# A two-layer hybrid decoder trunk on one core: the first input split into high and low parts k-tile by k-tile, and lambda computed behind the indexer

## The chip, the cores and the metric

The kernel runs on one core of one Trainium2 chip. Five engines work side by side, each through its own queue in order: TensorE (PE, matmuls; its weight loads are shown as PEld), VectorE (DVE), ScalarE (ACT), GpSimd (POOL) and SyncE (SP, which issues most DMAs). The metric is the device time of one execution in microseconds (us), as the median of several runs; lower is better.

## The reference, cut to what matters

Two pre-norm residual layers over 256 tokens of width 1024, in float32. Layer 0 mixes with indexed sparse attention and differential attention, layer 1 with native sparse attention; each is followed by a SwiGLU block.

```python
h = rmsnorm(x, norm_mix[layer])                 # x: (1, 256, 1024)
y = h @ ev_w_in[j]                              # layer 0: one projection, split by columns
qa_nope, qa_rope, c_kv, ka_rope, iq, ik, iw, qb, kb, vb = split_cols(y, EVEN_SPLITS)
o_a = dsa_mixer(...)                            # indexer scores, top-64 keys, latent attention
o_b = diff_mixer(qb, kb, vb, ev_lambda[j], ev_subln[j], lam_init, pos)
x = x + concatenate([o_a, o_b]) @ ev_w_out[j]
x = x + swiglu(rmsnorm(x, norm_ffn[layer]), w_gate, w_up, w_down)
```

In diff_mixer one number per layer, `lam_full = exp(sum(l0*l1)) - exp(sum(l2*l3)) + lam_init`, weighs the second softmax against the first.

## The kernel before, in words

Every float32 product is made of three fp32r matmuls: an operand a is split into a high part (a rounded copy) and a low part (a minus the high part), and act_hi·w_hi, act_hi·w_lo and act_lo·w_hi are summed in one PSUM bank (`mm3`, L330 to L332). So each weight tile takes one ACT instruction for `w_hi` (L110) and one DVE instruction for `w_lo` (L113), in `Weights.prepare`. Weight tiles arrive by SP's queue in the order of use, and up to six split tiles stand ahead of TensorE.

The layer's first input `x` (two row tiles t = 0, 1 of 128 tokens; eight k-tiles of 128 columns) is transposed on TensorE, four k-tiles into one PSUM bank `pt_x` (there are two such banks), scaled by the norm's gain `gc0`, and split into `aW`. `first_half(t, h)` does this for one row tile and one half h of the k-tiles. For t = 0, h = 0 ACT and DVE work one k-tile at a time, straight from PSUM (L297, L298). For the three other halves DVE first writes the scaled half to SBUF as `xg` (L301, 512 columns), and ACT and DVE then split that (L240, L241). Behind it stand the sums of squares (L284, four on ACT), `rs` (L224 on DVE and a power on POOL, L225), and the first projection in chunks of 328, 416, 384 ... columns, in `project`: each chunk has four weight tiles of two k-tiles, so 48 matmuls. Each chunk's result is turned by `rope` (L390, L392, L395 on DVE).

The order on each engine is set by a scheduler that takes the program's order as priority and an instruction's readiness by its own costs; what is marked with `pin` (`keep_in_program_order`) keeps its place among the other pinned instructions of its engine. The scheduler also lets only one engine at a time at a PSUM bank, reads too: its waits are in the queue listings below as [waits ...].

`lam` (four small DVE instructions, L475, L476, L479 and L481, and one on ACT, L477) stands at the head of `even_mixer`. It is first used at L684, in differential attention.

Of the kernel before, what the change touches and what calls it, by code (L numbers as in the profile page):

```python
# [7 lines left out]
F32 = mybir.dt.float32  # L8
F32R = mybir.dt.float32r
BF16 = mybir.dt.bfloat16  # L10
AF = mybir.ActivationFunctionType
# [63 lines left out]
class Weights:  # L75
# [22 lines left out]
    def prepare(self, upto, behind=False):  # L98

        nc = self.tc.nc  # L100
        while len(self.ready) < min(upto, len(self.queue)):
            i = len(self.ready)
            self.load(i + 1)
            raw = self.raw[i]
            self.raw[i] = None
            _, kk, w = self.queue[i]
            n = kk * w
            hi = self.pool.tile([P, WCOLS], F32R, tag="hi", bufs=self.bufs[1], name="w_hi")
            lo = self.pool.tile([P, WCOLS], F32R, tag="lo", bufs=self.bufs[1], name="w_lo")
            act = nc.scalar.activation(hi[:, :n], raw[:, :n], AF.Copy)  # L110
            if behind:
                self.tc.keep_in_program_order(act)
            nc.vector.tensor_sub(lo[:, :n], raw[:, :n], hi[:, :n])  # L113
            self.ready.append((hi[:, :n].rearrange("p (k c) -> p k c", k=kk), lo[:, :n].rearrange("p (k c) -> p k c", k=kk)))

    def next(self, hold=1):
# [8 lines left out]
def trunk(tc, x, w0, w1, sm0, cw, vec, gcol, cst, out, dbg=None):  # L125
# [159 lines left out]
            if h == 1:  # L285
                rsqrt_sum(self.rs[t], ms)

    def first_half(nm, t, h):

        pt = t_bank("pt_x").rearrange("p (k c) -> p k c", k=4)  # L290
        for i in range(4):
            TE.transpose(pt[:, i], xs[t][:, (4 * h + i) * P : (4 * h + i + 1) * P], ident)
        hi, lo = nm.aT[t]
        if t == 0 and h == 0:
            for k in range(4):
                g = gc0[:, k : k + 1]
                pin(A.activation(hi[:, k], pt[:, k], AF.Copy, scale=g))  # L297
                V.scalar_tensor_tensor(lo[:, k], pt[:, k], g, hi[:, k], op0=ALU.mult, op1=ALU.subtract)  # L298
        else:
            xg = nat("xg").rearrange("p (k c) -> p k c", k=4)  # L300
            V.tensor_mul(xg, pt, gc0[:, 4 * h : 4 * h + 4].unsqueeze(2).broadcast_to([P, 4, P]))  # L301
            split(hi[:, 4 * h : 4 * h + 4], lo[:, 4 * h : 4 * h + 4], xg)

    class Final:

# [153 lines left out]
    def even_mixer(nm, goff):  # L459
        aT, rs = nm.aT, nm.rs  # L460
        with tc.tile_pool(name="even", bufs=1, reuse_waits="tile") as pool:
# [6 lines left out]
            ukT, uv = sm[:, :512], sm[:, 512:]  # L468


            lamv = small[:, V_LAM - V_KV :].rearrange("p (a b d) -> p a b d", a=2, b=2)
            lp = pool.tile([P, 2, 64], F32, tag="lam_p", name="lam_p")
            l2 = pool.tile([P, 2], F32, tag="lam_2", name="lam_2")
            nlam = pool.tile([P, 1], F32, tag="nlam", name="nlam")
            V.tensor_mul(lp, lamv[:, :, 0], lamv[:, :, 1])  # L475
            V.tensor_reduce(l2, lp, axis=AX.X, op=ALU.add)  # L476
            A.activation(l2, l2, AF.Exp)  # L477
            lam_init = 0.8 - 0.6 * math.exp(-0.3 * 0)
            V.tensor_scalar(nlam, l2[:, 1:2], l2[:, 0:1], -lam_init, op0=ALU.subtract, op1=ALU.add)  # L479
            subg = pool.tile([P, P], F32, tag="subg", name="subg")  # L480
            V.tensor_scalar(subg, small[:, V_SUB - V_KV : V_SUB - V_KV + P], 1.0 - lam_init, None, op0=ALU.mult)  # L481


            iTs = [early("iT").rearrange("p (k c) -> p k c", c=T) for _ in range(2)]
            iw_ = early("iw").rearrange("p (a t c) -> p a t c", a=2, t=NT)
            wv = [pool.tile([P, 8], F32, tag=f"wv{t}", name="wv") for t in range(NT)]
# [51 lines left out]
            for t in range(NT):  # L538
# [21 lines left out]
                V.tensor_scalar(am, work, TAKEN / 2, NEG, op0=ALU.is_gt, op1=ALU.mult)  # L560
                V.tensor_add(am, am, mask(t))
                addm.append(am)


            for h in range(0, 8, 4):
# [373 lines left out]
        return nxt  # L939

    first = Norm(V_MIX0)
    for h in range(2):
        for t in range(NT):
            first_half(first, t, h)
            W.prepare(2 * h + t + 1, behind=(h,t)==(0,1))
    for t in range(NT):
        for h in range(2):
            first.square(t, h)
# [135 lines left out]
```

## Time and profile before

| | |
|---|---|
| runs | 660.07, 664.07, 663.41 us; median 663.41 us |
| profiled execution | 661.37 us, of which the span from first to last instruction is 659.7 us |
| PE busy | 644.5 us (98% of the span) |
| DVE busy | 489.8 us (74%) |
| ACT busy | 396.8 us (60%) |

Busy time is the union of an engine's instructions. In a timeline row the first number is the start in us from the span's start, the second the time to the end of the last of the row's instructions; an engine's next instruction starts a little before the one ahead ends when it waits for nobody. What stands in square brackets is the idle time of that engine before the row and who ended it.

### The profile page before, as it was taken

What the parts mean: (1) busy time and instruction counts of PE and PEld (TensorE: products, weight loads), DVE (VectorE), ACT (ScalarE), POOL (GpSimd) and SP (SyncE); (2) the same over time, 40 slices, a digit from 0 to 9 for tenths busy, and PEclk for the clock granted to TensorE, in tenths of its full rate; (3) what the DMA queues carried; (4) which work ended last, traced back from release to release, by engine and by line L of the source; (5) the groups of instructions that cost most, each with busy time, mean ns of one, the idle gap of its engine ahead of it and who ended that gap; (6) DMA issues with size and microseconds to landing.
All of it is one profiled execution on the core that took longest, in us unless ns stands there. A gap on an engine that the chain in (4) does not pass through costs nothing.

```text
span 659.7 us, 10029 instructions
## 1 busy us (share of the span) xinstructions
PE 644.5 (98%) x3512; PEld 538.0 (82%) x3512; DVE 489.8 (74%) x1133; ACT 396.8 (60%) x804; POOL 12.9 (2%) x26
## 2 busy tenths in 40 slices
PE   8999999999999999999999999989999999999995
PEld 6978888788888888888888787766888888888884
DVE  5999977758978787544689889896698777775424
ACT  6785758547755555433377598786585555554312
POOL 2000000000000000000000000000000000000000
PEclk9999999999999999999999999999999999999998
DMA  8844354137866666663297420510486555565501
GB/s 296 297 126 155 96 179 142 32 138 258 255 192 189 188 191 190 191 193 104 68 376 234 144 101 12 163 61 1 165 277 201 188 191 191 182 184 187 194 21 65
DMA packets 31729, 109.15 MB, mean 165 GB/s; under 512 B 3648, under 2 KB 3904, under 8 KB 31424
## 3 DMA queue, kind: packets, MB, share of 16 engines
q1 hardware_dynamic: 31104, 107.92, 50.9%
q10 hardware_dynamic: 576, 0.59, 0.3%
q8 instruction: 28, 0.46, 0.3%
q14 instruction: 21, 0.17, 0.1%
HBM read 107.46 MB, written 1.05 MB: 164 GB/s over the span
## 4 chain that ended last, share of the span: by engine, by line
PE 85%; DVE 5%; ACT 3%; DMA 3%; issue 2%; POOL 0%; SPq 0%; POOLq 0%; ACTq 0%; DVEq 0%
PE ps_g L437 12%; PE ps_u L437 12%; PE ps_out L331 7%; PE ps_out L330 7%; PE ps_out L332 7%; PE ps_u L438 6%; PE ps_g L438 6%; PE ps_in L331 5%; PE ps_in L330 4%; PE ps_in L332 4%; DMA w_raw<-in_w 2%; PE ps_o L933 2%; PE pt_p L917 2%; DVE w_lo L113 2%; PE ps_s L898 1%
## 5 line engine op out<-in xcount | busy, mean ns | idle before, releaser
L113 DVE TENSOR_TENSOR w_lo<-w_raw,w_hi 128x1024 fp32r<-128x1024 f32 (+5 forms) x200 | 234.9, 1181 | 93.6 <-ACT w_hi L110 91.1
L110 ACT ACTIVATE w_hi<-w_raw 128x1024 fp32r<-128x1024 f32 (+5 forms) x200 | 203.5, 1023 | 136.0 <-PE ps_out L332 57.6
L437 PE MATMUL ps_g<-aW,w_hi 128*128 128x512 f32 x352 | 124.6, 396 | 0.3 <-DVE aW L241 0.3
L437 PE MATMUL ps_u<-aW,w_hi 128*128 128x512 f32 x352 | 124.6, 396 | 0.0
L438 PE MATMUL ps_u<-aW,w_lo 128*128 128x256 f32 x352 | 98.7, 280 | 0.0
L438 PE MATMUL ps_g<-aW,w_lo 128*128 128x256 f32 x352 | 98.7, 280 | 0.0
L437 PEld LDWEIGHTS ps_g<-aW,w_hi 128*128 128x128 f32 x352 | 66.0, 188 | 16.5 <-DVE aW L241 0.9
L437 PEld LDWEIGHTS ps_u<-aW,w_hi 128*128 128x128 f32 x352 | 66.0, 187 | 15.6 <-DVE hn L450 0.2
L330 PE MATMUL ps_in<-w_hi,aW 128*128 128x512 f32 (+5 forms) x208 | 76.9, 370 | 0.4 <-ACT aW L240 0.4
L331 PE MATMUL ps_in<-w_lo,aW 128*128 128x512 f32 (+5 forms) x208 | 77.0, 370 | 0.1
L332 PE MATMUL ps_in<-w_hi,aW 128*128 128x512 f32 (+5 forms) x208 | 76.0, 366 | 0.0
L331 PE MATMUL ps_out<-w_lo,hT_hi 128*128 128x512 f32 x176 | 69.2, 393 | 0.0
L332 PE MATMUL ps_out<-w_hi,hT_lo 128*128 128x512 f32 x176 | 69.0, 392 | 0.0
L330 PE MATMUL ps_out<-w_hi,hT_hi 128*128 128x512 f32 x176 | 68.7, 390 | 0.0
L438 PEld LDWEIGHTS ps_g<-aW,w_lo 128*128 128x128 f32 x352 | 66.5, 189 | 0.0
L438 PEld LDWEIGHTS ps_u<-aW,w_lo 128*128 128x128 f32 x352 | 66.5, 189 | 0.0
L400 ACT ACTIVATE e<-e,bias 128x128 f32<-128x128 f32 (+1 forms) x96 | 42.4, 446 | 2.6 <-DVE bias L399 2.6
L330 PEld LDWEIGHTS ps_in<-w_hi,aW 128*128 128x128 f32 x208 | 39.7, 191 | 4.8 <-ACT aW L240 0.6
L331 PEld LDWEIGHTS ps_in<-w_lo,aW 128*128 128x128 f32 x208 | 39.6, 190 | 4.7 <-issue 0.5
L332 PEld LDWEIGHTS ps_in<-w_hi,aW 128*128 128x128 f32 x208 | 39.5, 190 | 4.6 <-issue 0.5
L330 PEld LDWEIGHTS ps_out<-w_hi,hT_hi 128*128 128x128 f32 x176 | 33.0, 188 | 7.5
L331 PEld LDWEIGHTS ps_out<-w_lo,hT_hi 128*128 128x128 f32 x176 | 33.1, 188 | 7.0
(225 smaller groups left out, 892.4 us busy)
## 6 DMA issues: line engine op xcount, KB each, us to landing
w_raw<-in_w SPq DMA_DIRECT2D x176, 512.0 KB, 4.3
w_raw<-in_w SPq DMA_DIRECT2D x8, 384.0 KB, 4.5
gain<-in_vec SPq DMA_DIRECT2D x4, 512.0 KB, 4.6
cw<-in_cw SPq DMA_DIRECT2D x2, 1024.0 KB, 8.2
w_raw<-in_w SPq DMA_DIRECT2D x4, 416.0 KB, 5.3
w_raw<-in_w SPq DMA_DIRECT2D x4, 328.0 KB, 5.0
w_raw<-in_w SPq DMA_DIRECT2D x4, 304.0 KB, 2.7
x<-in_x SPq DMA_DIRECT2D x4, 256.0 KB, 5.1
```

Of the source, the lines that this page charges most:

```text
L110: act = nc.scalar.activation(hi[:, :n], raw[:, :n], AF.Copy)
L113: nc.vector.tensor_sub(lo[:, :n], raw[:, :n], hi[:, :n])
L330: TE.matmul(ps, act[0][:, k], wh, start=start, stop=False)
L331: TE.matmul(ps, act[0][:, k], wl, start=False, stop=False)
L332: TE.matmul(ps, act[1][:, k], wh, start=False, stop=stop)
L400: A.activation(e, e, AF.Exp, scale=-1.0, bias=bias, accum_out=den)
L437: TE.matmul(dst[f], wh[:, i, c], wide[:, k].rearrange("p z q -> p (z q)"), start=k == 0, stop=False)
L438: TE.matmul(dst[f][:, :T], wl[:, i, c], wide[:, k, 0], start=False, stop=k == KD - 1)
L898: mmi = TE.matmul(sb[:, i], qS[t][:, h], kz[:, par, :, :ns], start=z == 0, stop=z == 1)
L917: TE.transpose(pt[:, i, b, st], e[:, i, b, st * P : (st + 1) * P], ident)
L933: pin(TE.matmul(ob[64 * par : 64 * par + 64], vv[:, st, c : c + 64], pTs[par][:, b, st].rearrange("p j c -> p (j c)"), start=False, stop=l ...
```

## The change

The first input is split k-tile by k-tile in all four halves, from the transposes in PSUM; `xg` and the instructions L301, L240 and L241 go from this place. The transposes, the splits and the first four weight splits, on ACT and on DVE, are all pinned in a written order: tile 0, then t = 0 k-tiles 0 to 3, t = 1 k-tiles 0 and 1, weight tile 1, t = 1 k-tiles 2 and 3, and for the second half k-tiles 4 and 5 of both row tiles, weight tile 2, k-tiles 6 and 7 of both, weight tile 3. The sums of squares stand behind as before. The lambda instructions move from the head of `even_mixer` to behind the indexer.

```diff
-            act = nc.scalar.activation(hi[:, :n], raw[:, :n], AF.Copy)
+            parts = [nc.scalar.activation(hi[:, :n], raw[:, :n], AF.Copy), nc.vector.tensor_sub(lo[:, :n], raw[:, :n], hi[:, :n])]
             if behind:
-                self.tc.keep_in_program_order(act)
-            nc.vector.tensor_sub(lo[:, :n], raw[:, :n], hi[:, :n])
+                for part in parts:
+                    self.tc.keep_in_program_order(part)
...
-    def first_half(nm, t, h):
+    def first_turn(t, h):
 
         pt = t_bank("pt_x").rearrange("p (k c) -> p k c", k=4)
         for i in range(4):
-            TE.transpose(pt[:, i], xs[t][:, (4 * h + i) * P : (4 * h + i + 1) * P], ident)
+            pin(TE.transpose(pt[:, i], xs[t][:, (4 * h + i) * P : (4 * h + i + 1) * P], ident))
+        return pt
+
+    def first_split(nm, pt, t, h, ks):
+
         hi, lo = nm.aT[t]
-        if t == 0 and h == 0:
-            for k in range(4):
-                g = gc0[:, k : k + 1]
-                pin(A.activation(hi[:, k], pt[:, k], AF.Copy, scale=g))
-                V.scalar_tensor_tensor(lo[:, k], pt[:, k], g, hi[:, k], op0=ALU.mult, op1=ALU.subtract)
-        else:
-            xg = nat("xg").rearrange("p (k c) -> p k c", k=4)
-            V.tensor_mul(xg, pt, gc0[:, 4 * h : 4 * h + 4].unsqueeze(2).broadcast_to([P, 4, P]))
-            split(hi[:, 4 * h : 4 * h + 4], lo[:, 4 * h : 4 * h + 4], xg)
+        for i in ks:
+            k = 4 * h + i
+            g = gc0[:, k : k + 1]
+            pin(A.activation(hi[:, k], pt[:, i], AF.Copy, scale=g))
+            pin(V.scalar_tensor_tensor(lo[:, k], pt[:, i], g, hi[:, k], op0=ALU.mult, op1=ALU.subtract))
...
     first = Norm(V_MIX0)
+
+    W.prepare(1, behind=True)
     for h in range(2):
-        for t in range(NT):
-            first_half(first, t, h)
-            W.prepare(2 * h + t + 1, behind=(h,t)==(0,1))
+        pts = [first_turn(t, h) for t in range(NT)]
+        if h == 0:
+            first_split(first, pts[0], 0, h, range(4))
+            first_split(first, pts[1], 1, h, (0, 1))
+            W.prepare(2, behind=True)
+            first_split(first, pts[1], 1, h, (2, 3))
+        else:
+            for ks in ((0, 1), (2, 3)):
+                for t in range(NT):
+                    first_split(first, pts[t], t, h, ks)
+                W.prepare(3 + ks[0] // 2, behind=True)
```

On ACT's queue, from the first weight split to the first sum of squares, before (`pt_x_104` is the transposes of t = 0, first half; `xg_126` and `xg_139` are t = 1, first half and t = 0, second half):

```order
L110 ACTIVATE w_hi_117<-w_raw_88 128x656 [waits DMAHW2_49]
L297 ACTIVATE aW_101<-pt_x_104,gc0_75 128x128 [waits DMAHW4_49,PE_49]
L297 ACTIVATE aW_101<-pt_x_104,gc0_75 128x128 [waits DVE_49]
L240 ACTIVATE aW_101<-xg_126 128x4x128 [waits DVE_49]
L297 ACTIVATE aW_101<-pt_x_104,gc0_75 128x128 [waits DVE_49]
L110 ACTIVATE w_hi_130<-w_raw_91 128x656 [waits DMAHW5_49]
L240 ACTIVATE aW_101<-xg_139 128x4x128 [waits DVE_49]
L297 ACTIVATE aW_101<-pt_x_104,gc0_75 128x128 [waits DVE_49]
L110 ACTIVATE w_hi_143<-w_raw_95 128x656 [waits DMAHW0_49]
L110 ACTIVATE w_hi_156<-w_raw_97 128x656 [waits DMAHW1_49]
L284 ACTIVATE sq_161,ms2_160<-x0_67 128x512
```

And after, from the same weight split on (108 and 113 are the first halves of t = 0 and 1, 138 and 143 the second):

```order
L110 ACTIVATE w_hi_104<-w_raw_88 128x656 [waits DMAHW2_49]
L301 ACTIVATE aW_101<-pt_x_108,gc0_75 128x128 [waits DMAHW4_49,PE_49]
L301 ACTIVATE aW_101<-pt_x_108,gc0_75 128x128 [waits DVE_49] x3
L301 ACTIVATE aW_101<-pt_x_113,gc0_75 128x128 [waits PE_49]
L301 ACTIVATE aW_101<-pt_x_113,gc0_75 128x128 [waits DVE_49]
L110 ACTIVATE w_hi_130<-w_raw_91 128x656 [waits DMAHW5_49]
L301 ACTIVATE aW_101<-pt_x_113,gc0_75 128x128 [waits DVE_49] x2
L301 ACTIVATE aW_101<-pt_x_138,gc0_75 128x128 [waits PE_49]
L301 ACTIVATE aW_101<-pt_x_138,gc0_75 128x128 [waits DVE_49]
L301 ACTIVATE aW_101<-pt_x_143,gc0_75 128x128 [waits PE_49]
L301 ACTIVATE aW_101<-pt_x_143,gc0_75 128x128 [waits DVE_49]
L110 ACTIVATE w_hi_156<-w_raw_95 128x656 [waits DMAHW0_49]
```

Four k-tile instructions and three half-tile ones have become 16 k-tile ones, each of which waits for DVE unless it opens a new bank; the fourth weight split, `w_hi_168`, and the squares stand behind all 16.

On DVE's queue, from the third weight split to the first one of the second chunk (`w_lo_207`, 128x832), before:

```order
L113 TENSOR_TENSOR w_lo_144<-w_raw_95,w_hi_143 128x656 [waits DMAHW0_49,Activation_49]
L301 TENSOR_TENSOR xg_152<-pt_x_147,gc0_75 128x512 [waits PE_49]
L113 TENSOR_TENSOR w_lo_157<-w_raw_97,w_hi_156 128x656 [waits DMAHW1_49,Activation_49]
L224 TENSOR_SCALAR rs_102<-ms2_160 128x1 [waits Activation_49]
L224 TENSOR_SCALAR rs_103<-ms2_167 128x1 [waits Activation_49]
L475 TENSOR_TENSOR lam_p_178<-small_70 128x128 [waits DMAHW3_49]
L481 TENSOR_SCALAR subg_185<-small_70 128x128
L476 TENSOR_REDUCE lam_2_179<-lam_p_178 128x2 [waits DVE_49]
L241 TENSOR_TENSOR aW_101<-xg_152,aW_101 128x4x128 [waits Activation_49]
L390 SCALAR_TENSOR_TENSOR n0_288<-ps_in_202,rs_102,con_69 128x320 [waits DMAHW2_49,PE_49,Pool_49]
L479 TENSOR_SCALAR nlam_180<-lam_2_179 128x1 [waits Activation_49]
L113 TENSOR_TENSOR w_lo_207<-w_raw_204,w_hi_206 128x832 [waits DMAHW4_49]
```

And after (`w_lo_210` is the same first split of the second chunk):

```order
L302 SCALAR_TENSOR_TENSOR aW_101<-pt_x_138,gc0_75,aW_101 128x128 [waits Activation_49] x2
L302 SCALAR_TENSOR_TENSOR aW_101<-pt_x_143,gc0_75,aW_101 128x128 [waits Activation_49] x2
L110 TENSOR_TENSOR w_lo_157<-w_raw_95,w_hi_156 128x656 [waits DMAHW0_49,Activation_49]
L302 SCALAR_TENSOR_TENSOR aW_101<-pt_x_138,gc0_75,aW_101 128x128 [waits Activation_49] x2
L302 SCALAR_TENSOR_TENSOR aW_101<-pt_x_143,gc0_75,aW_101 128x128 [waits Activation_49] x2
L110 TENSOR_TENSOR w_lo_169<-w_raw_97,w_hi_168 128x656 [waits DMAHW1_49,Activation_49]
L224 TENSOR_SCALAR rs_102<-ms2_172 128x1 [waits Activation_49]
L390 SCALAR_TENSOR_TENSOR n0_291<-ps_in_205,rs_102,con_69 128x320 [waits DMAHW2_49,PE_49,Pool_49]
L224 TENSOR_SCALAR rs_103<-ms2_179 128x1 [waits Activation_49]
L392 SCALAR_TENSOR_TENSOR rope_b_292<-ps_in_205,rs_102,con_69 128x5x32 x2
L110 TENSOR_TENSOR w_lo_210<-w_raw_207,w_hi_209 128x832 [waits DMAHW4_49,Activation_49]
```

The lambda instructions are gone from here; two rope instructions (L392) now stand ahead of the second chunk's first `w_lo`, where before one (L390) did.

## Rows read from the trace of the kernel before

**Rows 1.** The page: busy time of TensorE, and the chain that ended last.

```profile
PE 644.5 (98%) x3512; PEld 538.0 (82%) x3512; DVE 489.8 (74%) x1133; ACT 396.8 (60%) x804; POOL 12.9 (2%) x26
PE 85%; DVE 5%; ACT 3%; DMA 3%; issue 2%; POOL 0%; SPq 0%; POOLq 0%; ACTq 0%; DVEq 0%
```

**Rows 2.** Busy us of each engine in stretches of the span; column PEclk is granted clock.

```profile
core 0: us, PE busy (x) PEld busy (x) DVE busy (x) ACT busy (x) POOL busy (x), PEclk, DMA share, GB/s
10.00:15.00 5.00, 4.80 (x30) 4.07 (x28) 5.00 (x9) 4.41 (x11) 0.00 (x0) 1.00 0.98 344
15.00:20.00 5.00, 4.79 (x28) 4.46 (x28) 4.99 (x13) 4.83 (x9) 1.59 (x2) 1.00 0.67 183
50.00:60.00 10.00, 9.96 (x60) 9.30 (x59) 10.00 (x30) 5.67 (x8) 0.00 (x0) 1.00 0.39 122
436.00:440.00 4.00, 2.14 (x15) 1.87 (x16) 4.00 (x20) 3.74 (x13) 0.00 (x0) 1.00 0.40 131
655.00:659.70 4.70, 0.00 (x0) 0.00 (x0) 0.49 (x1) 0.72 (x1) 0.26 (x1) 0.52 0.29 112
```

**Rows 3.** Timeline of ACT at the start.

```profile
5.35 0.75 ACT L110 ACTIVATE w_hi<-w_raw 128x656 fp32r<-128x656 f32 x1 [2.67 <-DMA w_raw<-in_w]
6.00 0.35 ACT L297 ACTIVATE aW<-pt_x,gc 128x128 fp32r<-128x128 f32 x1
7.27 0.37 ACT L297 ACTIVATE aW<-pt_x,gc 128x128 fp32r<-128x128 f32 x1 [0.92 <-DVE aW L298]
12.66 0.62 ACT L284 ACTIVATE sq<-x 128x512 bf16<-128x512 f32 x1
15.64 0.88 ACT L110 ACTIVATE w_hi<-w_raw 128x832 fp32r<-128x832 f32 x1
```

**Rows 4.** Timeline of DVE and POOL at the start.

```profile
6.13 0.84 DVE L113 TENSOR_TENSOR w_lo<-w_raw,w_hi 128x656 fp32r<-128x656 f32 x1 [4.97 <-ACT w_hi L110]
6.89 0.34 DVE L298 SCALAR_TENSOR_TENSOR aW<-pt_x,gc,aW 128x128 fp32r<-128x128 f32 x1
...
14.30 0.83 DVE L113 TENSOR_TENSOR w_lo<-w_raw,w_hi 128x656 fp32r<-128x656 f32 x1
15.38 0.28 DVE L475 TENSOR_TENSOR lam_p<-small 128x128 f32<-128x128 f32 x1
15.41 1.59 POOL L225 TENSOR_TENSOR rs<-rs,half 128x1 f32<-128x1 f32 x2 [12.01 <-DVE rs L224]
15.91 0.68 DVE L241 TENSOR_TENSOR aW<-xg,aW 128x512 fp32r<-128x512 f32 x1
16.60 0.55 DVE L390 SCALAR_TENSOR_TENSOR n<-ps_in,rs,con 128x320 f32<-128x320 f32 x1
17.19 2.89 DVE L113 TENSOR_TENSOR w_lo<-w_raw,w_hi 128x832 fp32r<-128x832 f32 x3
21.22 0.38 DVE L392 SCALAR_TENSOR_TENSOR rope_b<-ps_in,rs,con 128x160 f32<-128x160 f32 x1
```

**Rows 5.** Timeline of PE: first chunk's matmuls, and the second chunk's with `w_lo`.

```profile
7.26 0.62 PE L330 MATMUL ps_in<-w_hi,aW 128*128 128x328 f32 x1
7.95 0.47 PE L332 MATMUL ps_in<-w_hi,aW 128*128 128x328 f32 x1
8.23 0.47 PE L330 MATMUL ps_in<-w_hi,aW 128*128 128x328 f32 x1
12.93 0.31 PE L330 MATMUL ps_in<-w_hi,aW 128*128 128x328 f32 x1
13.08 0.31 PE L331 MATMUL ps_in<-w_lo,aW 128*128 128x328 f32 x1
18.37 0.35 PE L331 MATMUL ps_in<-w_lo,aW 128*128 128x416 f32 x1
```

**Rows 6.** Longest waits of PE's weight loads, 17 to 130 us (total, times, longest).

```profile
PEld pt_c L530 <- DVE n L527: 0.7, 2, 0.4
...
PEld pt_p L605 <- DVE pd L687: 0.7, 1, 0.7
```

More of the change, by code (lines that the diff above doesn't have):

```diff
@@ L468, in even_mixer @@
             ukT, uv = sm[:, :512], sm[:, 512:]
[L471 to L481, printed above, removed]
             iTs = [early("iT").rearrange("p (k c) -> p k c", c=T) for _ in range(2)]
@@ L562, in even_mixer @@
                 addm.append(am)
+            lamv = small[:, V_LAM - V_KV :].rearrange("p (a b d) -> p a b d", a=2, b=2)
+            lp = pool.tile([P, 2, 64], F32, tag="lam_p", name="lam_p")
+            l2 = pool.tile([P, 2], F32, tag="lam_2", name="lam_2")
+            nlam = pool.tile([P, 1], F32, tag="nlam", name="nlam")
+            pin(V.tensor_mul(lp, lamv[:, :, 0], lamv[:, :, 1]))
+            V.tensor_reduce(l2, lp, axis=AX.X, op=ALU.add)
+            A.activation(l2, l2, AF.Exp)
+            lam_init = 0.8 - 0.6 * math.exp(-0.3 * 0)
+            V.tensor_scalar(nlam, l2[:, 1:2], l2[:, 0:1], -lam_init, op0=ALU.subtract, op1=ALU.add)
+            subg = pool.tile([P, P], F32, tag="subg", name="subg")
+            pin(V.tensor_scalar(subg, small[:, V_SUB - V_KV : V_SUB - V_KV + P], 1.0 - lam_init, None, op0=ALU.mult))
             for h in range(0, 8, 4):
```

## The prediction

> **What bounds the kernel now.** I read the page first: TensorE (PE) is busy 98% of the span and holds 85% of the chain that ended last [rows 1]. From the second chunk of the first projection on, a us that PE starts later is a us at the end, and work of the other engines costs nothing unless PE waits for it. The waits say how seldom that is: between 17 and 130 us the longest that a weight load waited is 0.7 us [rows 6]. So the question is when PE can enter the second chunk. The windows answer why it doesn't do so earlier: from 10 to 15 us VectorE (DVE) is busy 5.00 of 5.00 us, from 15 to 20 us 4.99, and ScalarE (ACT) 4.41 and 4.83 [rows 2]. The start is bound by the two engines that split operands, not by PE. The timelines give the pieces: the fourth weight split ends on DVE at 14.30 + 0.83 = 15.13 us and the last half-tile split at 16.59 [rows 4]; the second chunk's first `w_hi` starts at 15.64 [rows 3], its `w_lo` at 17.19 [rows 4], and PE meets that `w_lo` at 18.37 [rows 5].
>
> **What is removed and added.** By busy time DVE wins: three `xg` products and three half-tile subtractions of 0.68 us go (the row of L241; L301 reads as many columns), some 3 × 1.2 = 3.6 us where one follows another, and twelve k-tile instructions come. One takes 0.34 us, and 0.26 where it follows straight on, since the next starts 0.08 before the end (6.89 against 6.13 + 0.84) [rows 4]: 3.1 us. ACT's three half-tile copies become twelve k-tile ones of 0.35 [rows 3]. If both engines ran through, this would be a small gain. They don't: in the queue listing each k-tile copy waits for DVE, and each DVE instruction for its copy. The trace has one such place already: the second ACT k-tile stood idle for 0.92 us until DVE had done the first, which ended at 6.89 + 0.34 = 7.23, and started at 7.27 [rows 3, 4]. A half through `xg` paid no such turns, since only DVE read PSUM and ACT split one half while DVE did other work.
>
> A rule of the Trainium skill speaks against this change here (page "PSUM — Partial Sum Buffer", section "PSUM bank collisions raise a hardware error"): ScalarE and VectorE may not touch one bank's same partitions at once, reads included, so the turns can't be had away while both read the same bank; the 0.92 us is that rule as this program keeps it. With turns the sum is the one below, without them the one of rival two.
>
> **The sum.** One turn: 0.04 us to hand over to ACT, 0.36 for the copy, 0.03 back (6.13 against 5.35 + 0.75 = 6.10), 0.34 on DVE: 0.77 us [rows 3, 4]. Where the order opens a bank or follows a weight split, DVE goes straight on in 0.26. A weight split in between costs 1.15: `w_hi` of 0.75 starts 0.10 before its forerunner's end, `w_lo` of 0.84 comes 0.03 behind it, and DVE's last k-tile (0.37 with hand-over) lies beside it.
> From 7.23, the end of the first k-tile on DVE, which doesn't move, there are nine turns (three in the first bank, two in each of the others): 6.93 us; five instructions straight on: 1.30; weight splits two and three: 2.30; and the first k-tile of the fourth bank at some 0.6, an estimate, because its transposes wait on PE until the second bank is read and behind matmuls that need the second `w_lo`. That ends the splits at 7.23 + 11.13 = 18.36 us, and the fourth `w_lo` at 19.5, against 15.13 before.
> On ACT the fourth `w_hi` starts at 17.9 and the squares at 18.54; four at 0.62 [rows 3] give 21.02 for the second chunk's first `w_hi`, against 15.64. On DVE `rs` follows the second square at about 19.9, POOL's power takes half of 1.59 us [rows 4], so rope starts near 20.9; L390 (0.55) and two L392 (0.38 each), less overlaps, are 1.15 us with the other `rs`, and the second chunk's first `w_lo` runs from 22.05 to 23.05. PE meets it at 23.1 instead of 18.37: **4.7 us later**. Two matmuls of the second chunk stand ahead of it instead of one, which gives back 0.2 (328 columns take 0.15 us apart [rows 5], so 416 take 0.19).
> The pinned `w_lo` of tiles 2 to 4 have only the splits queued behind them on DVE, which is counted. The refills of raw tiles on SP wait for the same `w_lo` and come some 4 us later, but PE wants them that much later too; nothing.
> Lambda: four DVE instructions of about 0.28 each [rows 4] and one on ACT. Taking them from the start is in the times above. Behind the indexer they fall into a stretch where DVE is busy 10.00 of 10.00 us [rows 2], so 0 to 1.0 us could reach PE through the softmax; I take 0.3, near the lower end, because PE is busy 9.96 there: its work is queued ahead.
> Sum: 4.7 − 0.2 + 0.3 = **4.8 us** more. Nothing behind it gives it back: the FFN and the other layer are PE's. The ends: a turn of 0.69 (no hand-over at all) or 0.85 (twice the hand-over) moves nine turns by 0.7 each way, and lambda by −0.3 to +0.7, so 3.8 to 6.2.
> The profiled execution took 661.37 us, 2.0 below the median of 663.41, and the three runs lie on both sides of it. Added to the one it is 666.2, to the other 668.2; I take the middle, **667.2 us**. No change is 662.4 on that footing.
>
> **Rivals.**
> One, the late start is partly made good. PE then sits behind weights that are ready, and waits such as the 0.7 us on L527 and on L687 [rows 6] could vanish. They hang on chains that begin with PE's own results and so move along; against it also that DVE has no slack there. If 2 us come back: 665.2.
> Two, **faster**: the turns cost nothing, because DVE's load decides and the waits are met when asked. Then DVE needs 15 × 0.26 + 3 × 0.76 from 7.23, and the fourth `w_lo` ends at 13.4, 1.7 us earlier than before; through squares and rope some 1.4 us reach PE: 661.0. It decides only if a turn costs no more than an instruction that goes straight on, 0.26 us; the 0.92 us in [rows 3] speaks against it, as a wait that ends with DVE's end.
> Three, TensorE's clock falls. Between about 13.5 and 23 us PE would be busy for less than half of the time, in pieces of up to 2 us idle. The rows of before show both answers: with 2.14 of 4.00 us busy, at 436 to 440 us, the granted clock stayed at 1.00 (2.4 GHz); after PE's last matmul it stood at 0.52 on average, half of it being 1.2 GHz [rows 2]. At the lower level a 128x328 matmul takes 0.28 us (7.95 to 8.23) instead of 0.15 (12.93 to 13.08) [rows 5]. The last ten matmuls of the first chunk would then hold the rope back by 0.5 us, and if the second chunk runs as slowly as PE did from 7.26 to 9.9 us, half of 2.6 is lost: 1.8 on top, 669.0.
> The Trainium skill (page "TensorE: Matmul & The Clock Gate", part 1) has the clock granted by recent activity and taken back after idling, which is this rival; no row here shows PE at so thin a load for so long, so the trace neither confirms nor denies it.
>
> **How the numbers follow.** Forecast, the turns reach PE in full: 0.60, 665.2 to 669.6. Rival one 0.14, rival two 0.07, rival three 0.19, from 668 to 671 over its own ends. The range 663 to 671 takes in the first and third and nearly all of rival one; what lies outside is rival two and the far ends. A difference of 1% (6.6 us) is about what these runs can tell from no change. Slower by more than that means above 670.0: half of rival three and the forecast's upper edge, 0.17. Faster by over 1% would need more than PE's whole idle time at the start: 0.02. Within 1%: 0.81.
>
> **What would show it.** Right: the timeline of ACT alternates with DVE at about 0.77 us per k-tile from 7 to 18 us; ACT's k-tiles show idle time ended by L302, but for those that open a bank or follow a weight split; the second chunk's first `w_hi` starts near 21 us and PE meets its `w_lo` near 23; from there to the end PE's instructions lie some 4.8 us later at every mark, and the span is about 664.5. Wrong: if ACT and DVE overlap on one bank (rival two); if the shift shrinks between 25 and 130 us (rival one); if 128x416 matmuls behind 23 us stand 0.35 us apart (rival three). The sum fails at its first step if a turn is not 0.77, and at its last if PE loses its lead elsewhere.

## The result, and the profile after

The changed kernel takes 670.26 us, the median of four runs (669.07 to 671.37), against 662.09 for the kernel before on the same chip (four runs, 660.07 to 664.07): a ratio of 1.0119, with a 95% interval of 1.0086 to 1.0151, or 7.9 us more. The forecast was 667.2 in a range of 663 to 671. So the time lies in the range, the sign and the place were foretold, and the loss is 3.1 us larger than forecast; it lies above the forecast's own ends, 665.2 to 669.6. The profiled execution took 670.21 us with a span of 668.4, against 661.37 and 659.7.

The page of the changed kernel, the lines that answer to [rows 1]:

```profile
PE 647.0 (97%) x3512; PEld 539.0 (81%) x3512; DVE 491.0 (73%) x1139; ACT 398.9 (60%) x813; POOL 12.5 (2%) x26
PE 80%; DVE 7%; ACT 5%; DMA 4%; issue 2%; POOL 1%; POOLq 0%; SPq 0%; ACTq 0%; DVEq 0%
```

PE has 2.5 us more of busy time and 5 points less of the chain; what it lost went to DVE, ACT and a DMA. The windows of the changed kernel (busy us of each engine, then the granted clock) say where, to be read beside [rows 2]:

```profile
core 0: us, PE busy (x) PEld busy (x) DVE busy (x) ACT busy (x) POOL busy (x), PEclk, DMA share, GB/s
10.00:15.00 5.00, 5.00 (x26) 4.73 (x24) 2.42 (x6) 2.31 (x7) 0.00 (x0) 1.00 0.94 362
15.00:20.00 5.00, 2.53 (x14) 1.94 (x14) 2.94 (x8) 3.25 (x9) 0.00 (x0) 1.00 0.28 85
20.00:25.00 5.00, 3.45 (x17) 2.56 (x18) 3.75 (x8) 5.00 (x12) 1.11 (x2) 1.00 0.28 81
```

From 10 to 20 us DVE was full before (5.00 and 4.99 of 5 us); it is now busy for about half, and so is ACT to 15 us. PE, which lacked 0.2 us from 15 to 20 and nothing from 20 to 25, lacks 2.47 and 1.55 us there. Neither splitting engine is the bound any more: each waits for the other. The last of these stretches in the kernel before:

```profile
20.00:25.00 5.00, 5.00 (x30) 4.92 (x29) 5.00 (x13) 1.84 (x3) 0.00 (x0) 1.00 0.97 326
```

The timeline of the changed kernel, ACT first, then DVE, then PE:

```profile
7.22 0.37 ACT L301 ACTIVATE aW<-pt_x,gc 128x128 fp32r<-128x128 f32 x1 [0.92 <-DVE aW L302]
8.01 0.37 ACT L301 ACTIVATE aW<-pt_x,gc 128x128 fp32r<-128x128 f32 x1 [0.42 <-DVE aW L302]
...
14.79 0.37 ACT L301 ACTIVATE aW<-pt_x,gc 128x128 fp32r<-128x128 f32 x1 [1.36 <-PE pt_x L292]
...
19.06 0.74 ACT L110 ACTIVATE w_hi<-w_raw 128x656 fp32r<-128x656 f32 x1
19.70 0.62 ACT L284 ACTIVATE sq<-x 128x512 bf16<-128x512 f32 x1
...
22.16 3.98 ACT L110 ACTIVATE w_hi<-w_raw 128x832 fp32r<-128x832 f32 x5
...
8.41 0.35 DVE L302 SCALAR_TENSOR_TENSOR aW<-pt_x,gc,aW 128x128 fp32r<-128x128 f32 x1 [0.43 <-ACT aW L301]
...
13.47 0.35 DVE L302 SCALAR_TENSOR_TENSOR aW<-pt_x,gc,aW 128x128 fp32r<-128x128 f32 x1 [0.43 <-ACT aW L301]
15.19 0.35 DVE L302 SCALAR_TENSOR_TENSOR aW<-pt_x,gc,aW 128x128 fp32r<-128x128 f32 x1 [1.37 <-ACT aW L301]
...
19.20 0.35 DVE L302 SCALAR_TENSOR_TENSOR aW<-pt_x,gc,aW 128x128 fp32r<-128x128 f32 x1 [0.43 <-ACT aW L301]
19.83 0.84 DVE L110 TENSOR_TENSOR w_lo<-w_raw,w_hi 128x656 fp32r<-128x656 f32 x1 [0.28 <-ACT w_hi L110]
...
12.68 0.47 PE L331 MATMUL ps_in<-w_lo,aW 128*128 128x328 f32 x1
12.96 0.47 PE L332 MATMUL ps_in<-w_hi,aW 128*128 128x328 f32 x1
13.23 0.35 PE L331 MATMUL ps_in<-w_lo,aW 128*128 128x328 f32 x1
...
14.15 0.60 PE L292 MATMUL pt_x<-con,x 128*128 128x128 f32 x4
...
24.38 0.46 PE L331 MATMUL ps_in<-w_lo,aW 128*128 128x416 f32 x1 [0.65 <-DVE w_lo L110]
```

The turns are there: ACT's second and third k-tiles start at 7.22 and 8.01, 0.79 us apart, the idle time before each ended by L302, and a DVE k-tile that doesn't go straight on waits 0.43 us for L301. The fourth bank opens 1.72 us after the k-tile before it on DVE (13.47 to 15.19), because PE transposes for it only at 14.15, though DVE had read the bank's former content by 12.77. The splits end at 19.55, the fourth `w_lo` at 20.67, the four squares fill ACT from 19.70 to 22.16, and PE meets the second chunk's first `w_lo` at 24.38 where it was 18.37 [rows 5]: 6.0 us later. PE was also at the lower of its two clock levels for longer: matmuls of 328 columns still stand 0.27 us apart at 12.96, where before they stood 0.15 apart at 12.93 [rows 5]. The granted clock of that window reads 1.00 all the same; that 0.27 us goes with the lower level is read from e1 below, where matmuls of 328 columns stand 0.27 us apart from 17.23 to 17.50 at a granted clock of 0.50.

The shift grows afterwards. Matched one by one with the kernel before, the same instruction of PE lies 6.3 us later at the end of the second chunk (27.7 us before), 7.35 at 56.7 us, 7.7 at 105.7, 8.1 at 282 and 8.8 at 339 and to the end. The waits of PE in the changed kernel from 28 to 60 us (total, times, longest); the same view of before has none from 20 to 60 us:

```profile
PE pt_c L517 <- DVE n L514: 0.4, 1, 0.4
PE pt_c L517 <- DVE n L395: 0.4, 1, 0.4
PE pt_q L588 <- DVE nq L395: 0.4, 1, 0.4
...
```

### The profile page after: what moved, and what is told of

It is laid out like the page before. It is cut to its first block, busy times and chain, and to the rows that moved or that the text cites. A ratio compares the mean times of both kernels' runs of the same rounds, so it can differ in the third digit from the quotient of the medians.

```text
span 668.4 us, 10043 instructions
## 1 busy us (share of the span) xinstructions
PE 647.0 (97%) x3512; PEld 539.0 (81%) x3512; DVE 491.0 (73%) x1139; ACT 398.9 (60%) x813; POOL 12.5 (2%) x26
## 4 chain that ended last, share of the span: by engine, by line
PE 80%; DVE 7%; ACT 5%; DMA 4%; issue 2%; POOL 1%; POOLq 0%; SPq 0%; ACTq 0%; DVEq 0%
PE ps_u L437 12%; PE ps_g L437 11%; PE ps_out L331 7%; PE ps_out L330 7%; PE ps_out L332 7%; PE ps_u L438 6%; PE ps_g L438 6%; PE ps_in L331 4%; PE ps_in L330 4%; DMA w_raw<-in_w 4%; PE ps_in L332 4%; DVE w_lo L110 2%; PE ps_o L933 2%; PE pt_p L917 2%; ACT w_hi L110 2%
## 5 line engine op out<-in xcount | busy, mean ns | idle before, releaser
L330 PE MATMUL ps_in<-w_hi,aW 128*128 128x512 f32 (+5 forms) x208 | 77.4, 376 | 3.8 <-ACT w_hi L110 2.8
L331 PE MATMUL ps_in<-w_lo,aW 128*128 128x512 f32 (+5 forms) x208 | 77.0, 371 | 1.3 <-DVE w_lo L110 1.3
L332 PE MATMUL ps_in<-w_hi,aW 128*128 128x512 f32 (+5 forms) x208 | 77.3, 372 | 0.0
L331 PE MATMUL ps_out<-w_lo,hT_hi 128*128 128x512 f32 x176 | 69.3, 393 | 0.0
L331 PEld LDWEIGHTS ps_in<-w_lo,aW 128*128 128x128 f32 x208 | 40.0, 192 | 6.2 <-DVE w_lo L110 2.2
L331 PEld LDWEIGHTS ps_out<-w_lo,hT_hi 128*128 128x128 f32 x176 | 33.1, 188 | 7.0
```

What stands on the lines that cost most here:

```text
L330: TE.matmul(ps, act[0][:, k], wh, start=start, stop=False)
L331: TE.matmul(ps, act[0][:, k], wl, start=False, stop=False)
L332: TE.matmul(ps, act[1][:, k], wh, start=False, stop=stop)
```

## The experiments

Ratios are to runs of the kernel before taken beside each kernel; its medians lay between 662.09 and 663.52 us, and the us more are the ratio's excess over 1 times that median. "Entry" is the time at which PE meets the second chunk's first `w_lo` (L331, 416 columns) in the profile: 18.37 us before, 24.38 after. Each entry comes from one profiled execution, and their starts differ. e2 has the start of the kernel before, and its entry is 17.82. PE waited 0.45 to 1.98 us for the second row tile of `x`, and the four transposes of that tile took 1.11 or 1.12 us in the kernel before, the changed kernel, e1, e5 and e6, and 0.65 to 0.72 in the others, where TensorE was at the higher of its two clock levels earlier. What that is worth at the entry is read at e4: 1.1 us. The profiled executions of e3 (662.66 us), e4 (664.03) and e10 (660.47) were the fastest of their kernels, 3 to 6 us under the medians. So the us more weigh above the entries, and a difference of about 1 us between two entries needs a reason from the timeline.

| Kernel | Ratio and 95% interval | us more | Entry, us |
|---|---|---|---|
| the change | 1.0119 (1.0086 to 1.0151) | 7.9 | 24.38 |
| e1, lambda back at the head | 1.0111 (1.0086 to 1.0136) | 7.4 | 23.48 |
| e2, lambda's move alone | 1.0002 (0.9985 to 1.0019) | 0.1 | 17.82 |
| e3, four banks | 1.0044 (1.0024 to 1.0063) | 2.9 | 19.59 |
| e5, turns of half a k-tile | 1.0265 (1.0237 to 1.0293) | 17.6 | 33.24 |
| e4, two matmuls to fill PE | 1.0112 (1.0091 to 1.0133) | 7.4 | 23.26 |
| e6, weight split ahead of the squares | 1.0099 (1.0081 to 1.0118) | 6.6 | 22.29 |
| e7, e3 and e6 together | 1.0040 (1.0021 to 1.0060) | 2.6 | 18.23 |
| e8, written order, old splits | 1.0073 (1.0057 to 1.0090) | 4.8 | 20.68 |
| e12, e8 with the squares early | 1.0026 (1.0009 to 1.0044) | 1.7 | 17.75 |
| e11, k-tiles alone | 1.0027 (1.0003 to 1.0050) | 1.8 | 19.88 |
| e10, e3 with the squares early | 1.0005 (0.9988 to 1.0022) | 0.3 | 17.91 |
| e13, two banks in alternation | 1.0074 (1.0048 to 1.0100) | 4.9 | 22.16 |

### Lambda: e1 and e2

The first is the changed kernel with the eleven lines on lambda back where they were, the second the kernel before with them moved. From the diff of the first:

```diff
-            pin(V.tensor_mul(lp, lamv[:, :, 0], lamv[:, :, 1]))
...
+            V.tensor_mul(lp, lamv[:, :, 0], lamv[:, :, 1])
...
```

> The changed kernel with the lambda instructions back at the head of the even mixer; the split in turns stays. Theory (the turns of ScalarE and VectorE on one PSUM bank cost the time): the second chunk still starts some 5.5 to 6.5 us late, the lambda instructions fit into VectorE's idle turns, and the ratio to the kernel before is 1.008 to 1.012; if the part of the loss that grows between 30 and 60 us comes from lambda, it is 1 to 1.5 us less than the changed kernel. Rival (lambda behind the indexer is the main cost): ratio 1.000 to 1.004.

> The kernel before with the lambda instructions alone moved behind the indexer, pinned as in the change. Theory (turns): ratio 0.999 to 1.002. Rival (lambda): 1.006 or more.

With lambda back the loss stays (1.0111), and its move alone gives 1.0002. The move costs nothing that these runs can tell; the 0.3 us of the forecast wasn't there, and the first input is the whole of the case. In the profile of the first TensorE's clock fell in the thin stretch; its windows:

```profile
15.00:16.80 1.80, 1.04 (x5) 0.77 (x6) 1.25 (x3) 0.89 (x3) 0.00 (x0) 0.99 0.02 7
16.80:20.20 3.40, 3.40 (x13) 3.03 (x12) 2.02 (x5) 2.98 (x9) 0.00 (x0) 0.50 0.39 125
20.20:25.00 4.80, 3.55 (x19) 2.92 (x19) 3.76 (x7) 4.75 (x9) 1.11 (x2) 1.00 0.39 109
```

From 16.8 to 20.2 us the granted clock is 0.50, the 1.2 GHz level, behind a stretch with 1.04 of 1.80 us busy. This is rival three as it was drawn, in another kernel than the one it was drawn for; PE's entry, 23.48, is no later for it than in the changed kernel, but the clock had also risen earlier (matmuls of 328 columns stand 0.15 us apart from 10.62 us on, where the changed kernel's do from 13.41), so the price of the fall can't be read from it.

### The turns: e3 and e5

In one, neighbouring k-tiles come from different banks, with four banks open at once; in the other, each k-tile is split in two halves of 64 columns, so that there are twice as many turns:

```diff
-        pt = t_bank("pt_x").rearrange("p (k c) -> p k c", k=4)
+        pt = (s_bank if h else t_bank)("pt_x").rearrange("p (k c) -> p k c", k=4)
...
+    turns = (
+        ((0, 0, 0), (0, 0, 1), (1, 0, 0), (0, 0, 2), (1, 0, 1)),
+        ((0, 0, 3), (1, 0, 2), (0, 1, 0), (1, 0, 3), (1, 1, 0), (0, 1, 1), (1, 1, 1)),
+        ((0, 1, 2), (1, 1, 2), (0, 1, 3), (1, 1, 3)),
+    )
```

```diff
-            pin(A.activation(hi[:, k], pt[:, i], AF.Copy, scale=g))
-            pin(V.scalar_tensor_tensor(lo[:, k], pt[:, i], g, hi[:, k], op0=ALU.mult, op1=ALU.subtract))
+            for c in (slice(0, 64), slice(64, 128)):
+                pin(A.activation(hi[:, k, c], pt[:, i, c], AF.Copy, scale=g))
+                pin(V.scalar_tensor_tensor(lo[:, k, c], pt[:, i, c], g, hi[:, k, c], op0=ALU.mult, op1=ALU.subtract))
```

> The changed kernel with four PSUM banks for the transposes (the second half of the k-tiles takes two of the banks that the indexer uses later) and an order in which neighbouring k-tiles lie in different banks, so that ScalarE reads one bank while VectorE reads another. The same 16 + 16 split instructions, the same four weight splits and the lambda move. Theory (turns): VectorE's last k-tile ends near 15 us instead of 19.5, the second chunk meets its w_lo near 20 us instead of 24.4, and half to three quarters of the loss is gone: ratio 1.003 to 1.007. Rival (the number of instructions or the pinned order costs the time, not the waiting for a bank): 1.010 to 1.013.

> The changed kernel with each k-tile split in two pieces of 64 columns, so that ScalarE and VectorE take 32 turns instead of 16. Theory (turns): a 64-column turn is 0.6 to 0.7 us, so each k-tile costs some 0.5 us more where it waits, the second chunk starts 5 to 6 us later than in the changed kernel, and the ratio is 1.018 to 1.022. Rival (busy time of VectorE and ScalarE decides): 16 more instructions of about 0.2 us each at most, 3 us, ratio up to 1.016.

Four banks give back 5.0 of the 7.9 us by the medians, and the intervals are apart. The timeline of that kernel:

```profile
8.99 0.87 ACT L301 ACTIVATE aW<-pt_x,gc 128x128 fp32r<-128x128 f32 x3
...
9.88 0.86 DVE L302 SCALAR_TENSOR_TENSOR aW<-pt_x,gc,aW 128x128 fp32r<-128x128 f32 x3
...
10.52 0.88 ACT L301 ACTIVATE aW<-pt_x,gc 128x128 fp32r<-128x128 f32 x3 [0.66 <-DVE aW L302]
...
14.26 0.74 ACT L110 ACTIVATE w_hi<-w_raw 128x656 fp32r<-128x656 f32 x1
...
17.36 3.98 ACT L110 ACTIVATE w_hi<-w_raw 128x832 fp32r<-128x832 f32 x5
```

Both engines run through three k-tiles without a wait, and they overlap: DVE reads its bank from 9.88 to 10.74 while ACT reads another from 10.52. The splits are done when the fourth `w_hi` starts at 14.26, against 19.06 in the changed kernel. The Trainium skill (page "PSUM — Partial Sum Buffer", section "Specifications (TRN2)") says that ScalarE and VectorE can read PSUM side by side at full rate as long as the banks differ; the rows agree, with three k-tiles in 0.87 us. The second experiment, with twice the turns, loses another 9.7 us, nearly twice what was expected. Its ACT, and then its windows:

```profile
7.81 0.32 ACT L302 ACTIVATE aW<-pt_x,gc 128x64 fp32r<-128x64 f32 x1 [0.35 <-DVE aW L303]
...
30.04 3.98 ACT L110 ACTIVATE w_hi<-w_raw 128x832 fp32r<-128x832 f32 x5
...
20.00:25.00 5.00, 2.85 (x9) 2.48 (x10) 2.58 (x8) 2.69 (x9) 0.00 (x0) 0.56 0.20 53
25.00:30.00 5.00, 3.38 (x12) 2.59 (x11) 2.28 (x7) 3.94 (x13) 0.56 (x1) 0.50 0.17 44
```

A half turn takes 0.67 us there (7.14 to 7.81), within the 0.6 to 0.7 expected. All of ACT's waits between half tiles are for DVE and none is for PE, and the second chunk's first `w_hi` starts at 30.04 where it was 22.16: 7.9 us from turns alone. The clock stood at the lower level from 20.6 us on, and behind the splits that adds to it: the entry is 8.9 us later than in the changed kernel, the end of the second chunk 10.5. That turns set the time is shown by both.

### The late rise of the clock: e4

```diff
-            first_split(first, pts[0], 0, h, range(4))
+            first_split(first, pts[0], 0, h, range(3))
+            fill(first.aT[0][1][:, 2])
+            first_split(first, pts[0], 0, h, (3,))
```

> The changed kernel with two extra matmuls of 512 columns on TensorE behind the third k-tile of the first bank; their result is not used. They fill the idle time that the trace of after has from 8.96 to 9.47 us, ahead of the rise to full clock (first at 13.3 us there, at 10.1 before). Theory (the turns set the order, and the late rise adds about 1 us by holding back the fourth bank's transposes): full clock by about 10 us, the fourth bank's first k-tile on ScalarE near 13.7 instead of 14.8, and about 1 us back: 669.2, ratio to before about 1.010. Rival (the late rise is covered by the turns, PE has slack there): no change from after, 670.3, ratio 1.012. If TensorE stays at the lower level all the same, the run says nothing on the cost.

By time it is inconclusive: 1.0112, and the interval holds both values. Its profile shows the effect, though not by the added matmuls: PE's first matmuls of 328 columns stood 0.15 us apart from 7.85 us on, ahead of the added ones at 8.77. The fourth bank's first k-tile then started at 13.67 on ACT instead of 14.79, and the entry lay 1.1 us earlier. The timeline of this kernel, PE and then the two k-tiles of DVE around the opening of the fourth bank:

```profile
7.85 0.31 PE L337 MATMUL ps_in<-w_lo,aW 128*128 128x328 f32 x1
...
13.41 0.35 DVE L308 SCALAR_TENSOR_TENSOR aW<-pt_x,gc,aW 128x128 fp32r<-128x128 f32 x1 [0.43 <-ACT aW L307]
14.07 0.35 DVE L308 SCALAR_TENSOR_TENSOR aW<-pt_x,gc,aW 128x128 fp32r<-128x128 f32 x1 [0.31 <-ACT aW L307]
```

The fourth bank opens 0.66 us after the k-tile before it, where it took 1.72 us in the changed kernel. So in a profile with an early rise the late one's cost can be read, and it is the 1.1 us of the theory. In e1, without added matmuls, the same step takes 0.65 us. That the load, or the change, set the moment of the rise isn't shown.

### The squares: e6 and e7

In both kernels one line is added ahead of the squares, in the first to the change, in the second to the kernel with four banks:

```diff
+    W.prepare(5, behind=True)
     for t in range(NT):
         for h in range(2):
             first.square(t, h)
```

> The changed kernel with the second chunk's first weight split written ahead of the four sums of squares, nothing else. Theory (part of the loss is that the squares stand ahead of that split on ScalarE): its w_hi starts at 19.8 instead of 22.2 us and its w_lo ends near 21.7, so PE goes from the first chunk (which ends near 22.4) straight into the second: 128x416 on L331 at about 22.7 instead of 24.4, and 1.6 us come back: 668.7, ratio about 1.009. Rival (only the turns count, the squares lie beside them, or the rope that waits for rs takes their place): 670.3, ratio 1.012.

> Both at once: neighbouring k-tiles in different PSUM banks, and the second chunk's first weight split ahead of the squares. Theory (turns and the order of the squares are the whole loss at the start): against the run with four banks alone PE enters the second chunk 1.7 us earlier, near 17.8 us, about where the kernel before does (18.4): 664.3, ratio to before 1.001 (0.998 to 1.003). Rival (something else of the change costs 2 to 3 us, such as the written order of the weight splits on VectorE): it stays at 666.3, ratio 1.004.

Alone it gives back 1.3 us by the medians, near the 1.6 expected, though the two intervals don't separate it from the change. In the profile the entry comes 2.1 us earlier, as PE goes straight into the second chunk, and at 105.7 us 1.4 us of that are left. With four banks PE enters at 18.23, as early as the kernel before, and yet the ratio stays at 1.0040. The theory said 1.001 and fell; its rival, something else of 2 to 3 us, held. PE's waits from 28 to 60 us in this kernel say where most of it goes:

```profile
PE pt_c L517 <- DVE n L514: 0.9, 2, 0.7
PE pt_c L517 <- DVE n L395: 0.6, 1, 0.6
...
```

PE waits 1.5 us for what the rope writes on DVE (`n`), and its marks go from 0.2 us behind the kernel before at 27.7 us to 2.8 at 105.7.

### The written order alone: e8 and e12

The first is the kernel before, `xg` and all, with only the four weight splits in the written order on both engines. The second has the squares ahead of the last half besides:

```diff
-            act = nc.scalar.activation(hi[:, :n], raw[:, :n], AF.Copy)
+            parts = [nc.scalar.activation(hi[:, :n], raw[:, :n], AF.Copy), nc.vector.tensor_sub(lo[:, :n], raw[:, :n], hi[:, :n])]
...
+    W.prepare(1, behind=True)
...
-            W.prepare(2 * h + t + 1, behind=(h,t)==(0,1))
+            W.prepare(2 * h + t + 1, behind=True)
```

```diff
+            if (t, h) == (1, 1):
+                for m in range(4):
+                    first.square(m // 2, m % 2)
             first_half(first, t, h)
```

> The kernel before, with its half-tile splits through xg, but with the four weight splits in the written order of the change on both engines: the last half is then split ahead of the fourth weight tile, and all squares behind that. Theory (the written order costs only what the squares cost, the rest is the turns): the second chunk's first w_hi starts near 17.5 instead of 15.6 us, PE enters the second chunk about 1 us later, 664.5, ratio 1.0015 (1.000 to 1.004). Rival (the turns cost nothing that the order doesn't, the written order is the loss): ratio above 1.008. Second rival (the order is free): ratio 1.000 and the second chunk where it was.

> The run with the written order of the weight splits and the half-tile splits of before, with the four squares written ahead of the last half, into the 2.30 us that ScalarE stood idle there. Theory (the written order costs what it does, 1.0073, because the squares of 2.46 us were pushed behind the last weight split): second chunk's first w_hi near 16 instead of 18.4 us, PE enters the second chunk near 18.5, ratio 1.000 to 1.003, 663.5. Rival (the pinned w_lo on VectorE costs it, the squares don't): ratio stays at 1.006 to 1.008.

The written order alone costs 4.8 us without a single added turn, a ratio of 1.0073 where 1.0015 was expected, nearly five times the excess. The timeline of ACT in that kernel:

```profile
14.69 0.63 ACT L240 ACTIVATE aW<-xg 128x512 fp32r<-128x512 f32 x1 [2.30 <-DVE xg L301]
15.23 0.74 ACT L110 ACTIVATE w_hi<-w_raw 128x656 fp32r<-128x656 f32 x1
15.88 0.61 ACT L284 ACTIVATE sq<-x 128x512 bf16<-128x512 f32 x1
...
18.42 3.98 ACT L110 ACTIVATE w_hi<-w_raw 128x832 fp32r<-128x832 f32 x5
```

ACT stands idle for 2.30 us until DVE has the last half's `xg`, and does the squares afterwards. In the kernel before it did the squares in that very gap, from 12.66 us on [rows 3]. Put back there, as the second experiment does, they give back 3.1 of the 4.8 us, and the second chunk's `w_hi` starts at 14.99 instead of 18.42 (of these 3.4 us 1.0 is the earlier start of that execution: the last half's `xg` starts on DVE at 13.00 against 13.98). The theory held for about two thirds; 1.7 us are left, with an entry that is not late.

### The k-tiles without the order: e11 and e13

The first is the kernel before with all four halves split k-tile by k-tile, everything else left to the scheduler. The second is the changed kernel with its two banks, where only the written order alternates between them:

```diff
-        if t == 0 and h == 0:
-            for k in range(4):
...
-        else:
-            xg = nat("xg").rearrange("p (k c) -> p k c", k=4)
...
+        for i in range(4):
+            k = 4 * h + i
+            g = gc0[:, k : k + 1]
+            pin(A.activation(hi[:, k], pt[:, i], AF.Copy, scale=g))
+            V.scalar_tensor_tensor(lo[:, k], pt[:, i], g, hi[:, k], op0=ALU.mult, op1=ALU.subtract)
```

```diff
+        order = ((0, 0), (0, 1), (1, 0), (0, 2), None, (1, 1), (0, 3), (1, 2), (1, 3)) if h == 0 else ((0, 0), (1, 0), (0, 1), (1, 1), None, (0, 2), (1, 2), (0, 3), (1, 3))
+        for step in order:
+            if step is None:
+                W.prepare(2 + h, behind=True)
+            else:
+                first_split(first, pts[step[0]], step[0], h, (step[1],))
+    W.prepare(4, behind=True)
```

> The kernel before with all four halves split k-tile by k-tile from one bank each, lambda at the head and the order of the weight splits and squares left to the scheduler, which puts the squares between the k-tiles. Theory (turns and squares behind the splits add up: 7.9 us in all, 4.8 with the written order alone): turns of 0.77 to 0.79 us from 7 us on, the squares inside them, second chunk's first w_hi near 18.5 us, PE enters it some 3 us late: 666, ratio 1.003 to 1.006. Rival (the turns alone are the whole loss, the written order has its own price only without them): ratio 1.010 or more.

> The changed kernel with the same two PSUM banks and only the written order altered: the k-tiles of the two tokens' halves alternate from k-tile to k-tile, so neighbouring ones lie in different banks; squares behind the splits, lambda behind the indexer. Theory (walking through one bank after the other makes a full turn of each k-tile, and that is some 5 of the 7.9 us; the rest is the squares): two k-tiles per 0.79 us, the second chunk about 1 to 2 us late, ratio 1.003 to 1.006, as with four banks (1.0044). Rival (two banks don't do: the transposes of the second half wait until both are read, and TensorE's wait takes the place of the turns): ratio 1.008 or more.

The k-tiles alone cost only 1.8 us, a little less than I had expected, and in another way. The timeline of that kernel:

```profile
8.03 0.62 ACT L297 ACTIVATE aW<-pt_x,gc 128x128 fp32r<-128x128 f32 x2 [1.59 <-PE pt_x L292]
8.82 0.62 ACT L297 ACTIVATE aW<-pt_x,gc 128x128 fp32r<-128x128 f32 x2 [0.16 <-DVE aW L298]
9.61 0.63 ACT L297 ACTIVATE aW<-pt_x,gc 128x128 fp32r<-128x128 f32 x2 [0.16 <-DVE aW L298]
...
8.44 0.61 DVE L298 SCALAR_TENSOR_TENSOR aW<-pt_x,gc,aW 128x128 fp32r<-128x128 f32 x2 [1.12 <-ACT aW L297]
```

A turn still takes 0.79 us, but two k-tiles go through in each: the scheduler had both tokens' halves open and put their k-tiles alternately. That is read from the waits: ACT's second k-tile waits for transposes, so it is the other token's, and DVE reads from 8.44 us while ACT reads its next k-tile up to 8.65. So it isn't the split by k-tiles that costs a turn apiece, it is the order that walks through one bank before the next. The alternation by hand with two banks gave 1.0074, between theory and rival. Its timeline has both: pairs of k-tiles, and in between ACT waiting for the transposes of the second half:

```profile
12.17 0.37 ACT L301 ACTIVATE aW<-pt_x,gc 128x128 fp32r<-128x128 f32 x1 [0.89 <-PE pt_x L292]
13.35 0.62 ACT L301 ACTIVATE aW<-pt_x,gc 128x128 fp32r<-128x128 f32 x2 [0.81 <-PE pt_x L292]
```

These transposes have no third bank to go to while the first two are read. But that isn't the whole wait: DVE had read the first bank by 10.35 us, and PE transposed into it at 11.53, with matmuls of the first chunk ahead of it; the granted clock was 0.50 from 7.4 to 10.8 us. How much of the loss is the missing bank and how much this clock isn't shown.

### Both causes taken away: e10

The kernel with four banks, where the squares go into ACT's idle time between the k-tiles:

```diff
+    gaps = {(0, 0): (0, 0), (1, 2): (0, 1), (2, 1): (1, 0)}
...
+            if (n, m) in gaps:
+                first.square(*gaps[n, m])
...
+    first.square(1, 1)
```

> The changed kernel with four banks, and the sums of squares written into ScalarE's idle time (three of them between k-tiles, where the four-bank run waited 0.92, 0.66 and 0.65 us; the fourth behind the fourth w_hi). Theory (turns plus squares behind the splits are the loss at the start): the second chunk's first w_hi starts near 15.5 us and PE enters the second chunk no later than before (18.4 us); ratio 0.998 to 1.001, 662.0 to 663.5. Rival (the order that follows behind the second chunk, which changed in all these kernels, costs by itself): PE enters in time but comes later by about 2 us between 28 and 57 us, ratio 1.003 to 1.004.

The ratio is 1.0005 (0.9988 to 1.0022): as far as the interval tells the whole loss is gone, with the k-tile split and lambda behind the indexer still in place. The timeline of this kernel, ACT and then PE:

```profile
6.20 0.62 ACT L284 ACTIVATE sq<-x 128x512 bf16<-128x512 f32 x1
...
14.43 0.74 ACT L110 ACTIVATE w_hi<-w_raw 128x656 fp32r<-128x656 f32 x1
15.07 0.62 ACT L284 ACTIVATE sq<-x 128x512 bf16<-128x512 f32 x1
...
15.69 3.25 ACT L110 ACTIVATE w_hi<-w_raw 128x832 fp32r<-128x832 f32 x4
...
17.91 0.35 PE L331 MATMUL ps_in<-w_lo,aW 128*128 128x416 f32 x1
```

The first square runs at 6.20, while ACT would wait for DVE; the second chunk's `w_hi` starts at 15.69, where it was 15.64 before [rows 3]. PE enters as early as in the kernel before and in e2, and the time is no better than theirs.

## Why the prediction was right, and where its sizes were off

The chain of the prediction is the chain of the trace: turns, splits, fourth weight tile, squares, rope, second chunk. That the range holds the time is in part luck: the forecast's own ends stop at 669.6, and the range reaches 671 for rival three, a falling clock, which isn't what happened in the changed kernel's profile. Point by point:

- **The turn** was to be 0.77 us and is 0.79. Right.
- **The fourth bank's first k-tile** is the mis-sized term of the start. The prediction put it "at some 0.6, an estimate", and named the reason, the transposes that wait on PE. It took 1.72, since PE was at the lower clock level to about 13.2 us and its transposes came at 14.15. These 1.1 us, and 0.1 from the turns, carry the splits from the 18.36 foretold to 19.55, the fourth `w_lo` from 19.5 to 20.67, and the entry from 23.1 to 24.38. Where the clock rose earlier the 0.6 is right: the step takes 0.66 us in the profile of e4 and 0.65 in that of e1. What the term left out is that PE may still be at its lower level when the transposes are due.
- **The step "some 4.8 us later at every mark"** failed: between 27.7 us and the end another 2.5 us went, of which the forecast had 0.3, for lambda; the runs of lambda alone show none. The three waits of 0.4 us on DVE between 28 and 60 us, none of them there before, go with the first 1 us of it. Another 0.8 goes between 325 and 339 us, where PE waits 1.3 us for DVE's `nk` (L761) instead of 0.8. So the step of the prediction that nothing behind the second chunk changes the shift, as the rest is PE's, is what failed: PE met waits for DVE there that it hadn't before, and a longer one. The kernels with an entry as early as before but a changed order, e7 and e12, lose 2.6 and 1.7 us too. In e7 PE's waits for the rope show it. For e12 it isn't shown: its marks go from 0.6 us ahead of the kernel before at 27.7 us to 0.6 behind at 105.7, and the next 2.3 us are lost by 282 us, in the first FFN, of which the last section tells. So the order that the scheduler forms behind the written part costs 1 to 3 us in these profiles; e10, with an order no less changed, waits only 0.6 us for the rope between 28 and 60 us and doesn't lose them, and which of its differences does it stays open. That the shift grows, and at which waits, is shown; why the order behind makes them is only argued.
- **The turns alone as the cause** was half of the story. The sum held the squares (from 18.54 to 21.02; measured 19.70 to 22.16), but without saying that they were free before, in ACT's idle time, and are not any more. Without the turns the loss was 2.9 us, in the written order with the old splits it was 1.7 once the squares were back in their place, and with both causes taken away 0.3. The parts don't add up to the whole: the order alone costs 4.8 and the k-tiles alone 1.8, and the change, which has both, 7.9.
- **The rivals.** Rival one, a shift that shrinks, is refuted: it grew. Rival two, turns for nothing, is refuted by the 0.42 us that ACT stands idle before a k-tile. Rival three came nearest by its number, 669.0, and by half of its mechanism: in the changed kernel's profile the clock rose late and didn't fall, but in e1 and e5 it fell as drawn. The Trainium skill (page "TensorE: Matmul & The Clock Gate", part 1) has the clock granted by recent activity; the fall in e1's thin stretch agrees, while the thin load of the changed kernel, 2.53 of 5.00 us from 15 to 20, kept a granted clock of 1.00, so it isn't certain in any one execution.
- **The chances.** With 670.26 against 662.09 this is the "slower by over 1%" that had 0.17. In the traces the shift at the end is 8.8 us: 4.5 that the forecast had at the end of the second chunk, 1.3 more at the entry (1.1 of them at the fourth bank), 0.5 within the second chunk, and 2.5 behind it. The medians lie 8.2 apart.

## What to carry to other kernels

When two engines read the same data in turn, count the instructions that share a PSUM bank one after the other: each costs a full turn (0.79 us here for 128 columns, against 0.26 straight on). Let neighbours come from different banks, and see that enough banks are open for the transposes behind them (two in alternation still lost 4.9 us here, four 2.9). Before an order is written by hand, list what the free order did in the idle time of each engine: work that was free there, such as these squares of 2.46 us, gets a price when it is written behind the chain.

## What the hardware showed that was not expected

The same FFN matmuls ran at two speeds in the profiled executions at a granted clock of 1.00. The groups of PE from 170 to 250 us, first in the changed kernel, then in e7 (busy us, mean ns of one):

```profile
L437 PE MATMUL ps_g<-aW,w_hi 128*128 128x512 f32 x115 | 40.2, 391 | 0.0
```

```profile
L437 PE MATMUL ps_g<-aW,w_hi 128*128 128x512 f32 x116 | 41.4, 399 | 0.0
```

Across the first FFN the marks of e7 thereby move from 2.8 us behind the kernel before (139 us) to 4.8 (282 us), with no wait in between; e8 and e12 do the same, while e3 keeps its place. In the first FFN the mean of this group is 391 to 394 ns in eight of the fourteen profiles and 399 in six; in the second it is 394 in e4 and e6 and 399 in the others. The kernel before has 391 ns in its first FFN and 399 in its second, so both speeds occur within one execution. Whether one kernel changes its speed from execution to execution isn't shown, since each was profiled once. Some 2 us per FFN is as much as many of the differences studied here, and may be a part of the scatter of the runs: those of e10 lie between 660.47 and 665.02 us.
